# One load queue with a fixed order for two SwiGLU output stages, block sums loaded in the gate stage, four subtractions on GpSimd

## The chip, the cores and the metric

The kernel runs on one core of a Trainium2 chip. Five engines of the core work side by side, each with its own list of instructions: TensorE (PE in the profile, with PEld for its weight loads), VectorE (DVE), ScalarE (ACT), GpSimd (POOL) and SyncE (SP), which here only issues transfers. An instruction waits until the semaphores that it names are reached, and what stands behind it on the same engine waits with it. DMA transfers can be issued by SyncE and by ScalarE too; on either, an issue is a row of that engine's list, and the profile calls the two lists SPq and ACTq. The metric is the device time of one execution in microseconds (us).

## The reference, cut to what matters

The program is one decoder block on 1040 tokens (16 learned ones ahead of 1024) of width 1024, all in float32: a half-step SwiGLU, a mixer of two branches, a second half-step SwiGLU, and a final norm.

```python
def _swiglu(x, w_gu, w_down):              # w_gu (1024, 5632), w_down (2816, 1024)
    gate, up = jnp.split(x @ w_gu, 2, axis=-1)
    return (jax.nn.silu(gate) * up) @ w_down

h = h + 0.5 * _swiglu(_rmsnorm(h, ffn1_norm), ffn1_w_gu, ffn1_w_down)
u = _rmsnorm(h, mix_norm)                  # the mixer's input
...                                        # the mixer: h = h + merged @ w_out
h = h + 0.5 * _swiglu(_rmsnorm(h, ffn2_norm), ffn2_w_gu, ffn2_w_down)
return _rmsnorm(h, final_norm)[:, N_META:]
```

The change touches the last product of each SwiGLU, `(silu(gate) * up) @ w_down`, and the step from the first of them to the norm `u` of the mixer.

## The kernel before, in words

The kernel keeps activations transposed: a tile has 128 channels on its partitions and tokens along the row. The residual stream h is 8 such tiles, called h0 to h7 (hh0 to hh7 in the second SwiGLU).

**Precision.** A float32 product is made from three reduced ones. `split` (L162 to L164) writes a high part of a tile on ScalarE (L163) and the rest, source minus high part, on VectorE (L164, a subtraction with two inputs in the core's memory). Three matmuls, high by high, high by low and low by high, are summed in PSUM. Weights and activations are both split, so each weight tile costs ScalarE and VectorE one instruction each, and so does each activation tile.

**Stages.** The first SwiGLU has a gate stage (about 20 to 474 us of the span) and an output stage (474.6 to 717.5 us); then follows the mixer, called `middle`, whose first matmul starts at 721.9 us. The second SwiGLU has its gate stage up to 2781.8 us and its output stage from there to 3013 us; the final norm ends at 3028.2 us.

**The output stage.** `down` multiplies with a scheme that needs 7 products of half-size matrices where 8 are usual. A round r (0 to 6) is one of the 7. Its activation factor is one of the 7 forms in `FORMS` (t4, t1, t2, b22, b11, t3, b21), made of 11 tiles; its weight factor is a block of w_down or a sum of blocks, 4 row blocks m of 11 tiles of 128x128 each, in two chunks of 6 and 5 tiles (768 and 640 columns). So a round is 4 products, and a product has 66 matmuls in the first SwiGLU (two column halves of 256 and 264 tokens) or 33 in the second (512 tokens). At the end of a product VectorE adds the result to one or more h tiles (L707, "h add" below).

**Block sums.** The buffer `wsum` holds one round's weight factor for all four m. Rounds 0 and 4 load a block of w_down straight into it. Rounds 1, 2, 3 and 5 load another block into one of two buffers `wraw`, and GpSimd adds or subtracts it into `wsum` (L241). Round 6 needs a plain block and uses `wraw` alone; so does row block 0 of round 0. `loadw` then splits the chunk into a tile `w` for TensorE, and `fetchw` starts a load some chunks ahead of its use. A program written out once (`weight_order`) fixes the order of the chunks.

**Forms.** The gate stage makes the 7 forms of each of 11 tile columns k and stores them in device memory (`frm`, L523). The output stage brings them back, into slots that earlier rounds have used: `Hidden.load` issues the loads (L674, on ScalarE's list), `Hidden.split` splits them (L163 and L164 again), and `Hidden.step` says before each product how far both may go. A slot is free once the last product of the round that read it has used it. The very last form of the gate stage is split straight from the tile that holds it (`direct`), without a trip through memory.

**Residual.** `residuals` loads the h tiles, 260 KB halves, ahead of products of round 0 and, for four of them, of round 3 (L815 in the first SwiGLU, L925 in the second), on SyncE, as are the weights.

**What sets the order.** Each engine's list is fixed when the program is built. The order in which the Python code issues instructions is one input; a scheduler then places each instruction, and `issue_after` pins one instruction behind another. Before, the weight loads are chained to each other so, and the residual and `wsum` loads are pinned behind a weight load, while the form loads stand where the scheduler puts them on ScalarE's list, between the splits. Transfers of SyncE and ScalarE share eight completion semaphores in turn, so that each transfer's issue also waits for the one eight before it, from whichever list that came.

**The switch.** Behind the last round of the first SwiGLU, `hooks.after` squares h for the norm's sum (ACT L319, added up by GpSimd into `nsq`, L326), makes the normed tiles `nt` (DVE L866, two buffers) and splits each into `uk`, the mixer's input (`u_tile`). The mixer's first projection then reads `uk` (tile `pp`, L306), and a column sum over `nsq` on TensorE (`nps`, L337) belongs to the norm of the second half of the tokens.

Of the kernel before, what the change touches and what calls it, by code (L numbers as in the profile page):

```python
# [13 lines left out]
P = 128  # L14
# [202 lines left out]

def down_weights(g, name, raw, r, m, k0, kk):

    blk = lambda i, j: g.a[name][m + HK * i][:, HF * j + k0 : HF * j + k0 + kk]  # L220

    def dma(t, i, j):
        with ExitStack() as behind:
            if g.wdma and t is not raw:
                behind.enter_context(g.tc.issue_after(g.wdma.ins))
            ins = g.nc.sync.dma_start(t, blk(i, j))
        if t is raw:
            g.wdma = ins

    if r == LAST or (r == 0 and m == 0):  # L230
        dma(raw, *((0, 1) if r else (1, 1)))
        return raw
    s = g.wsum[:, m, k0 : k0 + kk]
    if r in (0, 4):
        dma(s, r == 0, r == 0)
        return s
    if r == 1 and m == 0:
        dma(s, 1, 1)
    dma(raw, *((1, 0), (0, 0), (0, 1), None, (1, 0))[r - 1])
    x, y = (raw, s) if r == 3 else (s, raw)  # L240
    g.nc.gpsimd.tensor_tensor(s, x, y, op=ALU.add if r == 1 else ALU.subtract)  # L241
    return s


def fetchw(g):
# [6 lines left out]
    if not down or idx[0] not in (0, 4) or idx[:2] == (0, 0):  # L252
        raw = g.wp.tile([P, KD, P], F32, name="wraw", tag="wraw", bufs=2)[:, :kk]
# [367 lines left out]
class Hidden:  # L621


    def __init__(self, g, n, pools):
        self.g, self.n, self.pools, self.loads, self.at = g, n, pools, [], {}
        self.order = [(r, p) for r in range(len(FORMS)) for p in range(HF)]
# [9 lines left out]
    def ahead(self):  # L636
        g = self.g
        g.wcount, g.wdma, g.held, g.direct = 0, None, [], self.direct
# [5 lines left out]
        fetchw(self.g)  # L644
# [6 lines left out]
        yield  # L651
        self.split(8)
        yield
        fetchw(self.g)
        self.split(HF - 1)
        yield
# [10 lines left out]
    def load(self, upto, done):  # L667
        while len(self.loads) < min(upto, len(self.slots)):
# [4 lines left out]
            if i != HF - 1:  # L673
                self.g.nc.scalar.dma_start(t[:, 1, :].bitcast(F32), self.g.frm[rp][:, : self.n])  # L674
# [13 lines left out]
def down(g, hs, which, n, hidden, hooks):  # L688
# [20 lines left out]
    for r in range(len(FORMS)):  # L709
        cols = halves(n)  # L710
        kept = {}
        for m in range(HK):
            hidden.step(r, m)
            hooks.before(r, m)

            def w(k0):
                kept[m, k0] = loadw(g, f"wdn{which}", r, m, k0)
                return kept[m, k0]
# [42 lines left out]
def ffn1(g):  # L761
    tc, nc = g.tc, g.nc
    n = T // 2
    with ExitStack() as ctx:
# [31 lines left out]
        hidden = Hidden(g, n, pools)  # L796
        g.wthird = ctx.enter_context(tc.tile_pool(name="wd", bufs=1, reuse_waits="tile"))
# [5 lines left out]
        hs = {k: sp.tile([P, T], F32, name=f"h{k}") for k in (3, 7, 2)}  # L803
        sum_tile = lambda shape, dtype: sp.tile(shape, dtype, name="wsum", tag="wsum", bufs=1)
        g.wsum = sum_tile([P, HK, HF, P], F32)
        hs.update({k: sp.tile([P, T], F32, name=f"h{k}") for k in (6, 5, 1, 0, 4)})
        spare = sp.tile([P, 2, ROW(n)], F32R, name="form")[:, :, :n]
        hidden.odd = hidden.places("t3", "22", "t4", "t1")
        hidden.arrange(spare, [])
        hooks = K()  # L810

        def residual(k, half):
            sl = slice(half * n, half * n + n)
            with tc.issue_after(g.wdma.ins):
                nc.sync.dma_start(hs[k][:, sl], g.a["hT"][k][:, sl])  # L815
# [3 lines left out]
        def before_last():  # L819
            early.close()  # L820
            t = sum_tile([P, 5, 2, ROW(n)], F32R)
# [8 lines left out]
            with tc.issue_after(g.wdma.ins):  # L830
                nc.sync.dma_start(g.ck, g.a["ck"][:, P:NSB])
# [18 lines left out]
        def after(r, m, s):  # L850
# [13 lines left out]
            for k, rs in hooks.todo[: 2 * s]:  # L864
                t = g.un.tile([P, 528], F32, name="nt", tag="nt", bufs=2)
                nc.vector.scalar_tensor_tensor(t, hs[k][:, SEGS[0][0] :], g.V("gm", k), rs, op0=ALU.mult, op1=ALU.mult)  # L866
                g.u.append(u_tile(g, t))
# [7 lines left out]
def ffn2(g):  # L875
# [3 lines left out]
    with ExitStack() as ctx:  # L879
# [28 lines left out]
        hidden = Hidden(g, n, pools)  # L908
        g.wthird = ctx.enter_context(tc.tile_pool(name="wd", bufs=1, reuse_waits="tile"))
# [4 lines left out]
        hs = {k: sp.tile([P, SEQ], F32, name=f"hh{k}") for k in (3, 7, 2)}  # L914
        g.wsum = sp.tile([P, HK, HF, P], F32, name="wsum", tag="wsum", bufs=1)
        hs.update({k: sp.tile([P, SEQ], F32, name=f"hh{k}") for k in (6, 5, 1, 0, 4)})
# [996 lines left out]
```

## Time and profile before

| | us |
|---|---|
| median of 3 runs | 3026.28 (3025.98 to 3031.26) |
| the profiled execution | 3030.14 |
| its span, first to last instruction | 3028.2 |
| PE busy in it | 2895.7 (96%) |
| DVE, ACT, POOL busy | 2165.3, 1438.0, 480.2 |
| first output stage, to the mixer's first matmul | 474.6 to 721.9 |
| second output stage | 2781.8 to 3013 |

The profiled execution is 3.9 us over the median, so differences are formed against its own time and then set off from the median. Instruction times count from the start of the span. Two columns of the stretch table matter most: how long PE was busy in a stretch, and PEclk, the mean clock that was granted to it (1.00 is full). "Idle before" in the timeline is the time for which an engine stood ahead of that instruction, with the instruction or transfer that ended it. A row of SPq or ACTq is a transfer's issue with the time for which it held its list; what it waits for holds up everything behind it there.

### The profile page before, as it was taken

The numbers are of one execution on the slowest core, as the hardware profiler recorded it, in microseconds if no ns is written. First come the engines' busy times: TensorE is split into PE (matmuls) and PEld (weight loads), VectorE is DVE, ScalarE is ACT, GpSimd is POOL, SyncE is SP. The second block draws the span as 40 slices with busy tenths as digits, with TensorE's granted clock in tenths as the row PEclk, the third lists the DMA queues.
The fourth block names the chain that finished last, engine by engine and source line by source line (L and its number), as shares of the span: only waits on it lengthen the run. The fifth ranks groups of instructions, "written<-read, shape, count | busy, mean of one in ns | idle before, by whom it ended". The sixth has DMA issues, their size and how long they took to land.

```text
span 3028.2 us, 62795 instructions
## 1 busy us (share of the span) xinstructions
PE 2895.7 (96%) x25630; PEld 2505.8 (83%) x25630; DVE 2165.3 (72%) x4083; ACT 1438.0 (47%) x2546; POOL 480.2 (16%) x550
## 2 busy tenths in 40 slices
PE   8999998999989999999998999999999999999998
PEld 8999998999877888888776777777777788887786
DVE  6566665866677877778868888777866766667675
ACT  5322223436655656556565655665644432224334
POOL 0332331412000000000000110000000033331520
PEclk9999999999999999999999999999999999999999
DMA  3333247644232322333332333233354233336662
GB/s 119 98 106 106 93 136 240 209 135 128 74 74 66 85 70 69 74 81 98 81 93 66 85 87 76 76 75 86 106 153 161 79 104 105 105 104 212 226 186 91
DMA packets 289727, 334.57 MB, mean 110 GB/s; under 512 B 172752, under 2 KB 178896, under 8 KB 289440
## 3 DMA queue, kind: packets, MB, share of 16 engines
q1 hardware_dynamic: 265744, 287.05, 31.8%
q10 hardware_dynamic: 23616, 43.33, 4.4%
q8 instruction: 201, 3.29, 0.5%
q14 instruction: 86, 0.70, 0.1%
q0 software_dynamic: 80, 0.19, 0.0%
HBM read 263.11 MB, written 67.38 MB: 109 GB/s over the span
## 4 chain that ended last, share of the span: by engine, by line
PE 46%; DVE 12%; ACT 5%; DMA 3%; issue 2%; POOL 1%; SPq 1%; DVEq 0%; ACTq 0%; POOLq 0%
PE pp L306 14%; PE pg L493 12%; PE pd L700 4%; PE pwo L306 3%; DVE w L164 2%; DVE tb L1575 1%; PE pg L517 1%; DVE Xb L1577 1%; ACT w L163 1%; DMA wraw<-in_wdn 1%; PE cs L1207 1%; PE vp L1260 1%; PE mp L1260 1%; DVE mt L1683 1%; PE np L1260 1%
## 5 line engine op out<-in xcount | busy, mean ns | idle before, releaser
L306 PE MATMUL pp<-uk,w 128*128 128x512 f32 (+2 forms) x4824 | 968.2, 346 | 13.8 <-DVE w L164 5.7
L306 PEld LDWEIGHTS pp<-uk,w 128*128 128x128 f32 x4824 | 742.5, 190 | 110.8 <-DVE w L164 13.0
L700 PE MATMUL pd<-form,w 128*128 128x256 f32 (+2 forms) x2652 | 432.0, 325 | 26.6 <-ACT w L163 14.7
L700 PEld LDWEIGHTS pd<-form,w 128*128 128x128 f32 x2652 | 388.3, 192 | 69.0 <-ACT w L163 15.5
L164 DVE TENSOR_TENSOR w<-wraw,w 128x1024 fp32r<-128x1024 f32 (+2 forms) x270 | 352.9, 1307 | 83.5 <-ACT w L163 79.9
L493 PE MATMUL pg<-bt,w 128*128 128x256 f32 (+2 forms) x2520 | 400.8, 317 | 0.2 <-DVE w L164 0.2
L493 PEld LDWEIGHTS pg<-bt,w 128*128 128x128 f32 x2520 | 360.2, 188 | 33.3 <-DVE w L164 0.6
L163 ACT ACTIVATE w<-wraw 128x1024 fp32r<-128x1024 f32 (+2 forms) x270 | 279.8, 1036 | 208.0 <-PE pg L493 127.7
L499 DVE TENSOR_TENSOR c<-c,pg 128x520 f32<-128x520 f32 (+1 forms) x280 | 189.4, 688 | 237.1 <-PE pg L493 213.0
L493 PE MATMUL pg<-b,w 128*128 128x256 f32 (+2 forms) x2160 | 347.8, 317 | 0.0
L493 PEld LDWEIGHTS pg<-b,w 128*128 128x128 f32 x2160 | 309.7, 188 | 28.1
L163 ACT ACTIVATE w<-wrx 128x1024 fp32r<-128x1024 f32 (+1 forms) x64 | 58.4, 912 | 281.5 <-PE pg L493 239.3
L163 ACT ACTIVATE w<-wsum 128x768 fp32r<-128x768 f32 x92 | 72.7, 791 | 228.1 <-PE pd L700 145.7
L463 POOL TENSOR_TENSOR wrx<-wrx 128x512 f32<-128x512 f32 x38 | 52.5, 1382 | 726.8 <-DVE w22b L164 548.9
L164 DVE TENSOR_TENSOR w<-wsum,w 128x768 fp32r<-128x768 f32 x92 | 95.9, 1048 | 85.7 <-ACT w L163 85.7
L1577 DVE TENSOR_TENSOR Xb<-Xb,tb 115x126 f32<-115x126 f32 (+22 forms) x496 | 125.2, 252 | 9.1 <-DVE tb L1575 0.4
L1575 DVE TENSOR_TENSOR tb<-Ub,Xb 115x126 f32<-115x126 f32 (+22 forms) x496 | 123.9, 250 | 9.3 <-DMA Ub<-scr 2.2
L1384 DVE SCALAR_TENSOR_TENSOR acc<-xr,pk,acc 128x528 f32<-128x528 f32 (+1 forms) x144 | 108.9, 757 | 29.3 <-ACT acc L1380 28.7
L241 POOL TENSOR_TENSOR wsum<-wsum,wraw 128x768 f32<-128x768 f32 (+1 forms) x48 | 93.2, 1955 | 229.1 <-DMA wsum<-in_wdn 106.6
L164 DVE TENSOR_TENSOR form<-form 128x512 fp32r<-128x512 f32 (+1 forms) x147 | 125.6, 900 | 2.0 <-ACT form L163 2.0
L306 PE MATMUL pwo<-uk,w 128*128 128x512 f32 x384 | 99.6, 412 | 4.1 <-DVE w L164 1.9
L163 ACT ACTIVATE form<-form 128x512 fp32r<-128x512 f32 (+1 forms) x147 | 83.0, 622 | 27.6 <-DMA form<-frm 11.6
(427 smaller groups left out, 4416.7 us busy)
## 6 DMA issues: line engine op xcount, KB each, us to landing
wraw<-in_win SPq DMA_DIRECT2D x150, 512.0 KB
wraw<-in_wgu SPq DMA_DIRECT2D x44, 512.0 KB
wrx<-in_wgu SPq DMA_DIRECT2D x44, 512.0 KB
frm<-c SPq DMA_DIRECT2D x76, 260.0 KB
frm<-c SPq DMA_DIRECT2D x76, 256.0 KB
form<-frm ACTq DMA_DIRECT2D x76, 256.0 KB
form<-frm ACTq DMA_DIRECT2D x71, 260.0 KB
wraw<-in_wdn SPq DMA_DIRECT2D x42, 384.0 KB
```

Source lines behind the costliest of these rows:

```text
L163: g.nc.scalar.activation(hi, src, AF.Copy)
L164: (eng or g.nc.vector).tensor_tensor(lo, src, hi.bitcast(F32), op=ALU.subtract)
L241: g.nc.gpsimd.tensor_tensor(s, x, y, op=ALU.add if r == 1 else ALU.subtract)
L306: g.nc.tensor.matmul(ps, lhsT=l, rhs=r, start=i == 0, stop=i == n - 1)
L463: sums.tensor_tensor(a22, a21, a22, op=ALU.add)
L493: nc.tensor.matmul(ps[:, c0 : c0 + cn], lhsT=l[:, x, k, :], rhs=r[:, k, y, c0 : c0 + cn], start=i == 0, stop=i == 3 * HK - 1)
L499: nc.vector.tensor_tensor(o, x, y, op=ALU.add)
L700: nc.tensor.matmul(pd[:, c0 : c0 + cn], lhsT=wd[:, u, k - k0, :], rhs=x[:, v, c0 : c0 + cn], start=k + i == 0, stop=k == HF - 1 and i == 2)
L1260: g.nc.tensor.matmul(ps[e][HS[dst], c0 : c0 + CB], lhsT=l, rhs=r, start=True, stop=True)
L1384: nc.vector.scalar_tensor_tensor(acc[:, :n], xr[:, tap : tap + n], V("convw", ct * 4 + tap), acc[:, :n], op0=ALU.mult, op1=ALU.add)
L1575: nc.vector.tensor_tensor(tv, U[:, i, i + 1 :].unsqueeze(2).to_broadcast([npt, nt, ncc]), X[:, i, 0:ncc].unsqueeze(1).to_broadcast([npt, n ...
L1577: nc.vector.tensor_tensor(X[:, i + 1 :, 0:ncc], X[:, i + 1 :, 0:ncc], tv, op=ALU.add)
```

## The change

1. A new helper `in_turn` issues a transfer from SyncE and pins it behind the one that it issued before. Within the output stages all loads go through it: the weights, the residual tiles, and the forms, which leave ScalarE's list. With this, 152 load rows leave ScalarE; SyncE's list is 1305 instead of 1173 rows. The order in which the code asks for the loads is now their order on the chip; the residual loads of a product come behind both weight chunks that are fetched in it.
2. `wsum` gets a pool of its own ("ws"), opened before the gate stage's inner part and no longer in the output stage's pool. `ahead`, which runs inside the gate stage, loads the four row blocks of round 0 into it, each as one transfer of 128x1408 (704 KB) instead of two. Row block 0 of round 0 is read from `wsum` too. Round 4 loads whole row blocks as well.
3. The pool of the third split weight tile ("wd") opens after the output stage's pool; the extra forms of the first SwiGLU's last round and the final norm's tiles take their room from the new pools.
4. At the switch the low parts of `uk` for odd k (4 of 8) are subtracted on GpSimd instead of VectorE.

The matmuls and their number stay as they were.

How this moves rows is seen at three places. The first is SyncE's list at the start of the first output stage, from the last store of a form on (`h_5068` and the like are h tiles; one load brings half of its tokens). Before:

```order
L523 DMA frm<-c_4920 128x520
L815 DMA h_5068<-in_hT 128x520
L815 DMA h_5065<-in_hT 128x520
L815 DMA h_5067<-in_hT 128x520
L815 DMA h_5068<-in_hT 128x520
L226 DMA wsum<-in_wdn 128x768
L226 DMA wsum<-in_wdn 128x640
L815 DMA h_5064<-in_hT 128x520
L815 DMA h_5066<-in_hT 128x520
L815 DMA h_5065<-in_hT 128x520
L226 DMA wsum<-in_wdn 128x768
L226 DMA wsum<-in_wdn 128x640
```

With the change, from the third row behind the last store on:

```order
L223 DMA h_5068<-in_hT 128x520
L223 DMA form<-frm 128x520 x3
L223 DMA h_5064<-in_hT 128x520
L223 DMA h_5066<-in_hT 128x520
L223 DMA h_5065<-in_hT 128x520
L223 DMA form<-frm 128x520 x3
L223 DMA h_5062<-in_hT 128x520
L223 DMA h_5063<-in_hT 128x520
L223 DMA h_5064<-in_hT 128x520
L223 DMA form<-frm 128x520 x2
L223 DMA wraw<-in_wdn 128x768
L223 DMA wraw<-in_wdn 128x640
```

The `wsum` loads are gone from here (they stand in the gate stage), form loads stand in their place, and the first `wraw` load of round 1 comes behind 18 residual and form loads.

The second place is ScalarE's list in rounds 0 and 1 of the same stage. Before:

```order
L163 ACTIVATE w<-wsum 128x640
L674 DMA form<-frm 128x520 x4
L163 ACTIVATE w<-wsum 128x768
L674 DMA form<-frm 128x520
L163 ACTIVATE form<-form 128x520 x4
L674 DMA form<-frm 128x520
```

With the change:

```order
L163 ACTIVATE w<-wsum 128x640
L163 ACTIVATE form<-form 128x520 x4
L163 ACTIVATE w<-wsum 128x768
L163 ACTIVATE form<-form 128x520 x2
L163 ACTIVATE w_5470<-wsum 128x640
L163 ACTIVATE form<-form 128x520 x2
```

The loads are gone from between the splits; the splits of four forms now stand ahead of the next chunk's split of weights.

The third place is VectorE's list at the switch, from the second normed tile on (`w<-wraw` is a weight of the mixer). Before:

```order
L866 SCALAR_TENSOR_TENSOR nt<-h_5066,pk,nrs 128x528
L164 TENSOR_TENSOR w<-wraw,w 128x1024
L164 TENSOR_TENSOR uk<-nt,uk 128x528 x2
L707 SCALAR_TENSOR_TENSOR h_5066<-pd,h_5066 128x256
L866 SCALAR_TENSOR_TENSOR nt<-h_5062,pk,nrs 128x528
L866 SCALAR_TENSOR_TENSOR nt<-h_5060,pk,nrs 128x528
L164 TENSOR_TENSOR uk<-nt,uk 128x528 x2
L866 SCALAR_TENSOR_TENSOR nt<-h_5068,pk,nrs 128x528
L707 SCALAR_TENSOR_TENSOR h_5062<-pd,h_5062 128x256
```

With the change, VectorE:

```order
L871 SCALAR_TENSOR_TENSOR nt<-h_5066,pk,nrs 128x528
L164 TENSOR_TENSOR w<-wraw,w 128x1024
L164 TENSOR_TENSOR uk<-nt,uk 128x528
L714 SCALAR_TENSOR_TENSOR h_5066<-pd,h_5066 128x256
L871 SCALAR_TENSOR_TENSOR nt<-h_5063,pk,nrs 128x528
L871 SCALAR_TENSOR_TENSOR nt<-h_5061,pk,nrs 128x528
L164 TENSOR_TENSOR uk<-nt,uk 128x528
L871 SCALAR_TENSOR_TENSOR nt<-h_5068,pk,nrs 128x528
L871 SCALAR_TENSOR_TENSOR nt<-h_5065,pk,nrs 128x528
L714 SCALAR_TENSOR_TENSOR h_5063<-pd,h_5063 128x256
```

and GpSimd, where the subtractions have gone between the sums of squares:

```order
L327 TENSOR_TENSOR nsq<-nsq 128x512 x4
L164 TENSOR_TENSOR uk<-nt,uk 128x528
L327 TENSOR_TENSOR nsq<-nsq 128x512
L164 TENSOR_TENSOR uk<-nt,uk 128x528 x2
L327 TENSOR_TENSOR nsq<-nsq 128x512
L164 TENSOR_TENSOR uk<-nt,uk 128x528
```

VectorE keeps every second low part; a normed tile `nt` that takes the buffer of an odd one now waits for GpSimd.

The diff, cut to what these points speak of:

```diff
+def in_turn(g, out, src):
+
+    with ExitStack() as behind:
+        if g.turn:
+            behind.enter_context(g.tc.issue_after(g.turn.ins))
+        g.turn = g.nc.sync.dma_start(out, src)
+
+
+def block(g, name, m, i, j, k0=0, kk=HF):
+    return g.a[name][m + HK * i][:, HF * j + k0 : HF * j + k0 + kk]
+
+
 def down_weights(g, name, raw, r, m, k0, kk):
 
-    ...
-    if r == LAST or (r == 0 and m == 0):
-        dma(raw, *((0, 1) if r else (1, 1)))
+    s = g.wsum[:, m, k0 : k0 + kk]
+    if r == 4 and k0 == 0:
+        in_turn(g, g.wsum[:, m], block(g, name, m, 0, 0))
+    if raw is None:
+        return s
+    i, j = ((1, 0), (0, 0), (0, 1), None, (1, 0), (0, 1))[r - 1]
+    in_turn(g, raw, block(g, name, m, i, j, k0, kk))
+    if r == LAST:
         return raw
-    s = g.wsum[:, m, k0 : k0 + kk]
-    if r in (0, 4):
-        dma(s, r == 0, r == 0)
-        return s
-    if r == 1 and m == 0:
-        dma(s, 1, 1)
-    dma(raw, *((1, 0), (0, 0), (0, 1), None, (1, 0))[r - 1])
     x, y = (raw, s) if r == 3 else (s, raw)
     g.nc.gpsimd.tensor_tensor(s, x, y, op=ALU.add if r == 1 else ALU.subtract)
     return s
...
     def ahead(self):
         g = self.g
-        g.wcount, g.wdma, g.held, g.direct = 0, None, [], self.direct
+        g.wcount, g.turn, g.held, g.direct = 0, None, [], self.direct
+        sums = lambda m: g.nc.sync.dma_start(g.wsum[:, m], block(g, self.name, m, 1, 1))
...
+        sums(0)
+        fetchw(g)
         self.split(3)
...
+        sums(1)
         self.split(8)
         yield
-        fetchw(self.g)
+        fetchw(g)
         self.split(HF - 1)
+        for m in (2, 3):
+            sums(m)
         yield
...
             if i != HF - 1:
-                self.g.nc.scalar.dma_start(t[:, 1, :].bitcast(F32), self.g.frm[rp][:, : self.n])
+                in_turn(self.g, t[:, 1, :].bitcast(F32), self.g.frm[rp][:, : self.n])
...
             hidden.step(r, m)
-            hooks.before(r, m)
 
             def w(k0):
                 kept[m, k0] = loadw(g, f"wdn{which}", r, m, k0)
+                if k0:
+                    hooks.before(r, m)
                 return kept[m, k0]
...
-        g.wthird = ctx.enter_context(tc.tile_pool(name="wd", bufs=1, reuse_waits="tile"))
+        wp = ctx.enter_context(tc.tile_pool(name="ws", bufs=1, reuse_waits="tile"))
+        g.wsum = wp.tile([P, HK, HF, P], F32, name="wsum", tag="wsum", bufs=1)
         with tc.tile_pool(name="gs", bufs=1, reuse_waits="tile") as sp:
             gu.send((hidden.ahead(), sp))
...
         hidden.arrange(spare, [])
+        g.wthird = ctx.enter_context(tc.tile_pool(name="wd", bufs=1, reuse_waits="tile"))
...
-                g.u.append(u_tile(g, t))
+                g.u.append(u_tile(g, t, nc.gpsimd if k % 2 else None))
...
-def u_tile(g, src):
+def u_tile(g, src, eng=None):
...
-    split(g, src, uk[:, 0, :], uk[:, 1, :])
+    split(g, src, uk[:, 0, :], uk[:, 1, :], eng)
     return uk
```

49 lines of the change are left out of this document (18 added, 31 removed).

## The prediction

> **What bounds the kernel now.** I read three views in turn: busy time by stretch (where does TensorE stop being busy?), its waits in those stretches (what ended them?), and the timeline at each (what was late, and for whom?). First the stretches of the two output stages; columns: length, PE busy with matmuls, PEld, DVE, ACT, POOL, granted clock, DMA share, GB/s.
>
> ```profile
> 474.50:520.00 45.50, 37.76 (x295) 36.85 (x294) 25.12 (x34) 14.68 (x23) 9.30 (x6) 0.92 0.82 290
> 520.00:560.00 40.00, 34.54 (x258) 33.80 (x257) 27.87 (x27) 12.03 (x19) 24.96 (x13) 0.91 0.65 201
> 560.00:600.00 40.00, 40.00 (x336) 40.00 (x336) 33.17 (x41) 19.27 (x32) 12.43 (x7) 1.00 0.71 237
> ...
> 2780.00:2820.00 40.00, 32.99 (x133) 26.30 (x132) 24.14 (x36) 15.48 (x24) 8.05 (x4) 0.87 0.88 305
> 2820.00:2860.00 40.00, 35.60 (x148) 28.30 (x147) 26.21 (x26) 11.11 (x18) 23.66 (x13) 0.96 0.65 208
> 2860.00:2900.00 40.00, 38.00 (x166) 30.65 (x165) 34.08 (x39) 16.84 (x28) 15.34 (x8) 1.00 0.73 231
> 2900.00:3013.00 113.00, 113.00 (x496) 92.71 (x495) 77.99 (x102) 48.25 (x73) 18.70 (x10) 1.00 0.38 120
> ```
>
> TensorE is the bound wherever it is full, and nothing here shortens a full stretch. Only the first 85 us of the first stage and the first 120 us of the second have idle time and a low clock. Full stretches also give the pace: 40.00/336 x 66 matmuls = 7.9 us per product of the first stage, 113.00/496 x 33 = 7.5 us in the second; a round of four is 31.5 and 30 us. TensorE's waits, 474 to 740 us, then 2780 to 3028 us:
>
> ```profile
> PE pd L700 <- ACT w L163: 7.6, 2, 6.3
> PE pd L700 <- DVE w L164: 4.5, 4, 2.5
> PE pp L306 <- DVE h L707: 4.4, 1, 4.4
> PE pd L700 <- ACT form L163: 0.8, 1, 0.8
> PE pd L700 <- DVE form L164: 0.4, 1, 0.4
> ```
>
> ```profile
> PE pd L700 <- ACT w L163: 7.0, 1, 7.0
> PE pd L700 <- DVE w L164: 6.4, 5, 3.1
> ```
>
> So 13.3 us of idle time in the first stage, 4.4 at the switch and 13.4 in the second. The timeline names what each stands for:
>
> ```profile
> 489.84 0.84 ACT L163 ACTIVATE w<-wsum 128x768 fp32r<-128x768 f32 x1 [5.50 <-DMA wsum<-in_wdn]
> 490.72 0.96 DVE L164 TENSOR_TENSOR w<-wsum,w 128x768 fp32r<-128x768 f32 x1 [4.96 <-ACT w L163]
> 490.74 0.80 PE L700 MATMUL pd<-form,w 128*128 128x256 f32 x2 [6.27 <-ACT w L163]
> ...
> 513.47 11.69 ACTq L674 DMA_DIRECT2D form<-frm  x4
> 525.28 0.84 ACT L163 ACTIVATE w<-wsum 128x768 fp32r<-128x768 f32 x1 [11.13 <-PE pd L700]
> 526.18 0.51 PE L700 MATMUL pd<-form,w 128*128 128x256 f32 x2 [1.38 <-ACT w L163]
> 528.29 3.11 PE L700 MATMUL pd<-form,w 128*128 128x256 f32 x16 [1.61 <-DVE w L164]
> 548.52 3.78 PE L700 MATMUL pd<-form,w 128*128 128x256 f32 x20 [2.47 <-DVE w L164]
> ...
> 2796.52 1.78 PE L700 MATMUL pd<-form,w 128*128 128x512 f32 x3 [7.01 <-ACT w L163]
> 2839.01 6.83 DVE L164 TENSOR_TENSOR form<-form 128x512 fp32r<-128x512 f32 x4
> 2846.63 8.68 PE L700 MATMUL pd<-form,w 128*128 128x512 f32 x30 [3.08 <-DVE w L164]
> ```
>
> The second product of round 0 waits in both stages for a block's transfer, 6.27 and 7.01 us. The stalls at 526 and 528 us come from ScalarE: four form loads held its list from 513.47 for 11.69 us, so the next weight split ran at 525.28. (The view puts that wait down to TensorE; 525.16 is where the fourth load was issued.) Those at 548 and 2846 us have another look: VectorE is late, and four form splits there took 6.83 us. Each stall is also paid in clock:
>
> ```profile
> 490.70:495.10 4.40, 4.17 (x18) 3.87 (x19) 2.70 (x4) 2.51 (x5) 0.00 (x0) 0.51 1.03 381
> 526.00:533.00 7.00, 5.21 (x28) 5.00 (x29) 6.24 (x7) 3.64 (x8) 4.25 (x3) 0.76 0.77 225
> 548.00:553.10 5.10, 4.58 (x25) 4.58 (x26) 3.72 (x5) 0.00 (x0) 4.56 (x2) 0.67 0.25 70
> 2796.50:2802.40 5.90, 5.88 (x14) 4.33 (x15) 4.97 (x7) 4.33 (x7) 0.00 (x0) 0.50 0.92 317
> 2834.00:2851.00 17.00, 12.60 (x46) 9.50 (x46) 17.00 (x16) 5.62 (x10) 12.07 (x7) 0.90 0.52 157
> ```
>
> Length times (1 - clock) is what the low clock cost: 2.2, 1.7, 1.7, 2.95 and 1.7 us. The Trainium skill (TensorE: Matmul & The Clock Gate, "What's actually happening") puts the half clock after about one idle window of some 3.4 us. The trace is stricter, since 2.47 us of idle at 548 us sufficed; by the page the sum below would lack the clock terms of the shorter stalls, about 3.4 us, and I go by the rows.
>
> **The change part by part.** *Block sums in the gate stage.* Round 0 no longer waits for its weights: 6.3 + 0.2 us in the first stage (the 0.2 is the next weight chunk's wait on VectorE) and 7.0 in the second, with 2.2 and 2.95 of clock. What it adds is four transfers of 704 KB early in the gate stage, 2.8 MB, some 10 us at the 290 GB/s above. That is hidden by slack there:
>
> ```profile
> DMA  3333247644232322333332333233354233336662
> L493 PE MATMUL pg<-bt,w 128*128 128x256 f32 (+2 forms) x2520 | 400.8, 317 | 0.2 <-DVE w L164 0.2
> ```
>
> The DMA engines are three tenths busy in the first slices (75.7 us each), and TensorE lost 0.2 us over 2520 matmuls of gate products. Without that cover a gate weight would come up to 10 us late, once per stage; below nothing is impossible, as the stage has no wait to win. I take 0.
>
> *The direct form.* The 0.8 + 0.4 us at the first stage's start come from ScalarE being busy with loads and form splits there. Its list is shorter now, but the form is still made last: between 0 and -1.2, I take -0.4.
>
> *Form loads off ScalarE.* The 1.4 + 1.6 us at 526 and 528 go, with 1.7 of clock, if the loads on SyncE don't hold what is needed sooner. At the stage's start SyncE issues 18 residual and form loads (each 128x520 floats; 4.8 MB together) ahead of round 1's first block: 16 us at 290 GB/s, from some 4 us into the stage on, so the block lands near 496, is added by 499 and split by 501; round 1 begins at 474.6 + 31.5 = 506. Slack 5 us, in the second stage some 4. Later, four form loads for round r+1 stand ahead of the weights and wait for the first tiles of round r's last product; the split of the weights for r+1's second product stands behind the splits of these forms on ScalarE. From the first freed slot to that product is 15.8 us (two products; 15 in the second stage). Needed: 2.9 us until four of eleven tiles are read, 2.5 for loads, 4 x 0.62 for ScalarE's splits, one VectorE split, then 0.84 + 0.96 for the weights, together some 10.4. Slack about 5 us again.
>
> *Who shares with whom.* VectorE and GpSimd hinder each other, and rounds 1, 2, 3 and 5 use both:
>
> ```profile
> 2841.48 1.87 POOL L241 TENSOR_TENSOR wsum<-wsum,wraw 128x768 f32<-128x768 f32 x1 [0.98 <-DMA wraw<-in_wdn]
> 2788.63 3.09 DVE L164 TENSOR_TENSOR form<-form 128x512 fp32r<-128x512 f32 x5
> ```
>
> A form split is 0.62 us alone and 1.71 us (6.83/4) beside GpSimd's sums. If they exclude each other, a round holds 4 x (1.87 + 1.56) on GpSimd (640 columns by five sixths), 4 x (0.96 + 0.80) of weight splits and 11 x 0.62 of forms: 13.7 + 7.0 + 6.8 = 27.5 us of 31.5 or 30. That fits, but tightly, and a late start isn't caught up. The stretch 560 to 600 us, with 33.17 of VectorE and TensorE full, says that it can go well; 2860 to 2900 us, with 34.08 and 2 us lost, that it need not. So of the stalls of this kind, 2.5 us at 548 and 6.4 in the second stage, I take half: 1.2 and 3.2, and half of their clock, 0.85 each. Bounds: none and all.
>
> *Four low parts to GpSimd.* At the switch TensorE waits for VectorE:
>
> ```profile
> 717.62 0.69 DVE L164 TENSOR_TENSOR uk<-nt,uk 128x528 fp32r<-128x528 f32 x1
> 718.01 1.44 POOL L326 TENSOR_TENSOR nsq<-nsq 128x512 f32<-128x512 f32 x1 [3.20 <-issue]
> 718.35 1.68 DVE L866 SCALAR_TENSOR_TENSOR nt<-h,pk,nrs 128x528 f32<-128x528 f32 x1
> 720.68 0.77 DVE L866 SCALAR_TENSOR_TENSOR nt<-h,pk,nrs 128x528 f32<-128x528 f32 x1
> 721.37 0.42 DVE L707 SCALAR_TENSOR_TENSOR h<-pd,h 128x256 f32<-128x256 f32 x1
> 721.93 4.19 PE L306 MATMUL pp<-uk,w 128*128 128x272 f32 x17 [4.43 <-DVE h L707]
> ```
>
> A normed tile takes 0.77 us alone and 1.68 beside GpSimd's addition, which takes 1.44. So a low part on GpSimd, 1.4 us by that row, shuts VectorE out, where it took 0.69 there: 4 x 0.7 = +2.8 if all is in series, less what the h adds (0.42, one input in PSUM) overlap. If they ran side by side, 4 x 0.69 = 2.8 would be won. The normed tiles, with two buffers, also wait for GpSimd now. The 0.91 us by which nt was longer decides for the first: +2.2. The Trainium skill says so too (SBUF — State Buffer, "SBUF: two separate sides": the pair of ports is an exclusive lock for a whole instruction); by it alone the term is the +2.8. The wait of 4.4 grows to some 6.6; late behind it is the mixer's first projection, which TensorE has nothing else to put before.
>
> *The sum.* First stage 6.5 + 0.4 + 3.0 + 1.2 + 2.2 + 1.7 + 0.85 = 15.9; second 7.0 + 3.2 + 2.95 + 0.85 = 14.0; switch -2.2. Together 27.7 us less: 3030.14 - 27.7 = 3002.4 for an execution like the profiled one, which is 3.9 us over the median of the runs: 2998.5.
>
> **The rivals.** *Rounds 1 and 2 keep their stalls*, since VectorE and GpSimd exclude each other and the form splits come no earlier. For it: 6.83 us for four splits. Against it: 560 to 600 us. Then only 6.5 + 2.2 + 7.0 + 2.95 - 2.8 = 15.9 are won: 3010. *Everything comes back*: all stalls and clock of both stages (18.8 and 18.1), the switch 2 us better, because GpSimd's work falls into VectorE's pauses: 39 less, 2987. Against it stands the nt row. *SyncE becomes the bound, and the kernel slower*: the four form loads wait for round r's last product, everything behind them with them, and the 5 us of slack are used up at each of five later rounds of both stages, for instance as VectorE's splits grow to 1.71 us and GpSimd's sums queue behind late blocks. A stall of 4 us with 1.7 of clock, ten times, is 57 against some 26 won: 3057. It decides above about 2.6 us a round; the slack worked out above speaks against it. *The sums come early but the gate stage pays*, with 5 us and clock in each: 3012; the 0.2 us row and the idle DMA engines speak against it. *The early sums don't land in time* because the buffer's room is freed late: round 0 waits as before and the rest gains 12 less 2: 3016.
>
> **How the numbers follow.** Forecast 0.52, stalls kept 0.17, all back 0.13, SyncE bound and slower 0.08, gate stage pays 0.06, sums late 0.04. The time is that of the first, 2998.5. The main case's own bounds are 2987 to 3010; with some microseconds of spread between runs and the middle rivals I go from 2985 to 3014. 0.2% is 6 us, about what a measurement tells from no change. Faster by more: all but the slower case and a part of the two middle ones, 0.87. Within 6 us: 0.05. Slower: 0.08.
>
> **What would show it.** Right: `w` splits of round 0 with no wait on a `wsum` transfer, TensorE full from 480 to 506 us, the ACTq rows of `form<-frm` gone and the stall at 526 us with them, clock 1.00 through 520 to 560 us, `uk<-nt` on POOL at about 1.4 us each, `pp` about 2 us later behind the last product. Wrong: waits for `wraw` or `form` on SPq's transfers in rounds 1 to 5, a gate stage that ends later than 474.6, or a switch that is shorter than 4.4 us.

## The result and the profile after

The changed kernel takes 3008.05 us (median of 5 runs, 3005.43 to 3014.11) where the kernel before took 3026.28: a ratio of 0.9939, 95% interval 0.9923 to 0.9955, so 18 us less with an interval of some 14 to 23. The forecast was 2998.5; the time lies in its range and the gain is two thirds of the one forecast. The profiled execution took 3009.62 us, its span is 3007.6 (before: 3028.2).

Where the 20.6 us between the two spans come from, by the first and last matmuls of the tiles pg, pd, pp and pwo (the mixer's last product) in both timelines (us); the second gate stage counts from the last pwo matmul, the mixer from the first of pp:

| stretch | before | after | difference | forecast |
|---|---|---|---|---|
| start and first gate stage | 474.6 | 473.9 | -0.7 | 0 |
| first output stage | 242.9 | 234.4 | -8.5 | -15.9 |
| switch, to the first pp matmul | 4.4 | 6.0 | +1.5 | +2.2 |
| mixer | 1630.9 | 1632.3 | +1.4 | 0 |
| second gate stage | 429.0 | 431.3 | +2.3 | 0 |
| second output stage | 231.2 | 214.7 | -16.5 | -14.0 |

The mixer is all but the same program in all kernels here, and in the fourteen profiles it took between 1628.8 and 1635.2 us (by the granted clock, 16 to 25 us of that were lost to half clock, more in one execution than in another); so a total that differs by 3 to 5 us says little, and most verdicts below go by the stretch that an edit touches.

TensorE's waits in the changed kernel, 474 to 740 us and then 2760 to 3010 us:

```profile
PE pd L707 <- DVE w L164: 7.2, 6, 2.3
PE pp L307 <- DVE h L714: 6.0, 1, 6.0
PE nps L338 <- POOL nsq L327: 0.8, 1, 0.8
PE pd L707 <- ACT w L163: 0.7, 2, 0.4
```

```profile
PE pd L707 <- DVE w L164: 2.0, 4, 0.7
PE pg L494 <- DVE w L164: 0.7, 1, 0.7
PE nps L338 <- ACT fin L320: 0.6, 1, 0.6
```

The long waits on ScalarE (7.6 and 7.0 us before) are gone in both stages. What is left of pd's waits is nearly all VectorE: 6.4 fell to 2.0 in the second stage, but 4.5 rose to 7.2 in the first. The stretches of the first stage (same columns as before):

```profile
474.50:520.00 45.50, 45.50 (x380) 45.30 (x379) 36.53 (x40) 20.01 (x31) 15.23 (x9) 1.00 0.85 285
520.00:560.00 40.00, 37.37 (x297) 36.96 (x296) 33.97 (x31) 13.75 (x20) 20.16 (x10) 0.96 0.49 156
560.00:600.00 40.00, 37.88 (x317) 37.67 (x316) 31.13 (x36) 13.79 (x21) 12.08 (x6) 1.00 0.51 182
600.00:640.00 40.00, 39.58 (x331) 39.38 (x330) 34.19 (x40) 18.40 (x28) 16.25 (x8) 1.00 0.68 227
640.00:680.00 40.00, 39.35 (x328) 39.31 (x328) 22.94 (x33) 14.88 (x23) 1.52 (x2) 1.00 0.48 159
```

The first 45.5 us are full at clock 1.00, as the forecast said. But 520 to 560 us still has a hole, and 560 to 680 us, which was full before, now has some too. The largest one, in the timeline of TensorE, VectorE and GpSimd around it:

```profile
519.77 2.43 DVE L164 TENSOR_TENSOR w<-wsum,w 128x768 fp32r<-128x768 f32 x1
522.12 4.93 DVE L164 TENSOR_TENSOR form<-form 128x520 fp32r<-128x520 f32 x3
526.97 2.15 DVE L164 TENSOR_TENSOR w<-wsum,w 128x640 fp32r<-128x640 f32 x1
...
519.54 4.08 POOL L242 TENSOR_TENSOR wsum<-wsum,wraw 128x768 f32<-128x768 f32 x2 [2.07 <-DMA wraw<-in_wdn]
524.56 1.93 POOL L242 TENSOR_TENSOR wsum<-wsum,wraw 128x768 f32<-128x768 f32 x1 [0.94 <-DMA wraw<-in_wdn]
526.78 1.66 POOL L242 TENSOR_TENSOR wsum<-wsum,wraw 128x640 f32<-128x640 f32 x1 [0.29 <-DMA wraw<-in_wdn]
...
518.32 0.72 ACT L163 ACTIVATE w<-wsum 128x640 fp32r<-128x640 f32 x1
...
529.18 1.06 PE L707 MATMUL pd<-form,w 128*128 128x256 f32 x5 [2.35 <-DVE w L164]
```

ScalarE is on time here: it began the high part of the 640-column chunk at 518.32, 8.65 us before VectorE began the low part. VectorE is behind: its weight splits take 2.43 and 2.15 us, and three form splits 4.93, each time beside a sum of GpSimd.

### The profile page after: what moved, and what is told of

The parts are those of the page before. It is cut to its first block, busy times and chain, and to the rows that moved or that the text cites. A ratio compares the mean times of both kernels' runs of the same rounds, so it can differ in the third digit from the quotient of the medians.

```text
span 3007.6 us, 62829 instructions
## 1 busy us (share of the span) xinstructions
PE 2890.0 (96%) x25630; PEld 2501.7 (83%) x25630; DVE 2194.8 (73%) x4079; ACT 1445.0 (48%) x2546; POOL 491.2 (16%) x554
## 4 chain that ended last, share of the span: by engine, by line
PE 50%; DVE 12%; ACT 5%; issue 2%; DMA 1%; SPq 0%; POOL 0%; DVEq 0%; ACTq 0%
PE pp L307 16%; PE pg L494 11%; PE pd L707 6%; PE pwo L307 3%; DVE w L164 2%; DVE tb L1581 1%; PE pg L518 1%; DVE Xb L1583 1%; ACT w L163 1%; PE cs L1213 1%; PE vp L1266 1%; PE mp L1266 1%; DVE mt L1689 1%; PE gra L1467 1%; PE np L1266 1%
## 5 line engine op out<-in xcount | busy, mean ns | idle before, releaser
L707 PEld LDWEIGHTS pd<-form,w 128*128 128x128 f32 x2772 | 396.7, 190 | 49.9 <-DVE w L164 12.3
L164 DVE TENSOR_TENSOR form<-form 128x520 fp32r<-128x520 f32 (+1 forms) x152 | 145.1, 991 | 13.0 <-ACT form L163 12.7
L164 DVE TENSOR_TENSOR w<-wsum,w 128x768 fp32r<-128x768 f32 x96 | 116.0, 1214 | 36.8 <-ACT w L163 36.8
L163 ACT ACTIVATE form<-form 128x520 fp32r<-128x520 f32 (+1 forms) x152 | 94.2, 632 | 77.1 <-DMA form<-frm 67.7
```

What stands on the lines that cost most here:

```text
L163: g.nc.scalar.activation(hi, src, AF.Copy)
L164: (eng or g.nc.vector).tensor_tensor(lo, src, hi.bitcast(F32), op=ALU.subtract)
L707: nc.tensor.matmul(pd[:, c0 : c0 + cn], lhsT=wd[:, u, k - k0, :], rhs=x[:, v, c0 : c0 + cn], start=k + i == 0, stop=k == HF - 1 and i == 2)
```

## The experiments

The theory at this point: VectorE and GpSimd exclude each other whenever both read their inputs from the core's memory; the first stage's remaining stalls, the longer switch, and a part of the old stalls that the forecast had put down to the form loads on ScalarE are all this one thing. The single rows of VectorE speak for it already: of 63 form splits of the first stage up to 680 us, 47 took 0.68 to 0.70 us and 16 took 1.91 to 2.35, with none between. So a split ran at its own pace there or was held up by most of a sum. The rivals: transfers that are late on SyncE's one list; the order of splits on VectorE; too few weight tiles.

**The same kernel once more**

> The changed kernel itself, as the base for the other three on this chip and to see how much its stretches differ between two executions. If the stalls of rounds 1 to 5 depend on how GpSimd's sums and VectorE's splits happen to meet, the first output stage differs by some microseconds from the 234.4 us of its first profile, with the stalls at other places; if they are set by the order of the loads alone, it repeats within 1 us. The time should be within 0.3% of 3008.

3013.2 us (3008.81 to 3015.08), ratio 0.9957 (0.9944 to 0.9970). The first output stage took 234.2 us, as before, but the stalls lay elsewhere: 2.03 us at 558, 1.00 at 634, 2.64 at 638 and only 0.31 at 526. The second took 212.2 (214.7). So the stage's length repeated, against what the theory expected of it, while the places moved, as it expected. That the length came out the same is chance: two kernels below whose rounds 1 to 5 are the same (low parts back on VectorE; early loads spread) took 237.8 and 240.4 us for the stage, with stalls of the same kind near 526 to 530, 562 to 565 and 634 to 645 us. The order of the loads, the same in all of them, doesn't set the stage's length by itself.

**GpSimd writes, but reads nothing**

```diff
-    g.nc.gpsimd.tensor_tensor(s, x, y, op=ALU.add if r == 1 else ALU.subtract)
+    for t in (raw, s, raw):
+        g.nc.gpsimd.memset(t, 0.0)
```

> The changed kernel with GpSimd's block sums replaced by three writes of zeros to the same tiles (about as long, but nothing is read, so the sums are left out). If the stalls left in the first output stage (2.35 us at 526.8, 2.12 at 562.6, 1.06 at 639.6) and the 2.0 us in the second come from VectorE and GpSimd excluding each other when both read, VectorE's splits are all 0.62 to 0.96 us, these stalls fall to under 1 us in all, and the time falls by 6 to 10 us. If they come from forms or blocks that land late on the one list of loads, or from too few weight tiles, they stay above 4 us.

This kernel leaves the sums out, so what it computes is of no use; its one execution took 3000.19 us. The first output stage falls from 234.4 to 227.5 us, the second from 214.7 to 211.4, and TensorE has no wait at all in rounds 1 to 5 of either; what stays, 2.7 us, is in the last round. The groups of the first stage, changed kernel and then this one (busy us, mean ns of one, idle before):

```profile
L164 DVE TENSOR_TENSOR form<-form 128x520 fp32r<-128x520 f32 x64 | 65.5, 1058 | 4.5 <-ACT form L163 4.4
L164 DVE TENSOR_TENSOR w<-wsum,w 128x768 fp32r<-128x768 f32 x23 | 29.6, 1288 | 0.8 <-ACT w L163 0.8
L242 POOL TENSOR_TENSOR wsum<-wsum,wraw 128x768 f32<-128x768 f32 x12 | 24.8, 2064 | 106.5 <-DMA wraw<-in_wdn 71.4 <-DVE h L714 31.5 <-DVE form L164 3.6
```

```profile
L164 DVE TENSOR_TENSOR form<-form 128x520 fp32r<-128x520 f32 x63 | 41.9, 696 | 7.5 <-ACT form L163 7.1
L164 DVE TENSOR_TENSOR w<-wsum,w 128x768 fp32r<-128x768 f32 x23 | 21.9, 952 | 1.7 <-ACT w L163 1.7
L243 POOL MEMSET wraw<- 128x768 f32 x32 | 23.7, 741 | 31.1 <-DMA wraw<-in_wdn 30.2
```

A form split takes 696 ns on average where it took 1058, a weight split 952 instead of 1288, although GpSimd is as busy as before (three writes of 741 ns for a sum of 2064). All 63 form splits up to 680 us now take 0.69 or 0.70 us; the group of 1.91 to 2.35 is gone. So neither GpSimd's time nor the loads are the cause, but what it reads. This is what the Trainium skill says (SBUF — State Buffer, "SBUF: two separate sides"): an instruction of VectorE with two inputs in that memory is locked out only by a GpSimd instruction that reads there.

**The sums on VectorE**

```diff
-    g.nc.gpsimd.tensor_tensor(s, x, y, op=ALU.add if r == 1 else ALU.subtract)
+    g.nc.vector.tensor_tensor(s, x, y, op=ALU.add if r == 1 else ALU.subtract)
```

> The changed kernel with all block sums on VectorE instead of GpSimd. If exclusion is what costs the stalls of rounds 1 to 5, a sum holds the shared inputs for 0.80 or 0.96 us instead of 1.57 or 1.87, VectorE and GpSimd need 20.8 instead of 27.5 us of a round in turn, and the idle time of both output stages falls from 8 and 0.2 to 2 us to about 3 (the last round's) and under 1; the first stage falls to some 229 us. If VectorE was the bound by its own work, with GpSimd beside it for free, its list grows by 7 us a round and the stalls grow to 10 us or more in each stage.

3001.36 us, ratio 0.9918 (0.9905 to 0.9931). The output stages take 227.1 and 211.4 us, no wait of TensorE is left in rounds 1 to 5, and 2.1 us in the last round; these are all the waits of pd, in the first stage (the second has none):

```profile
PE pd L707 <- ACT w L163: 1.7, 1, 1.7
PE pd L707 <- DVE w L164: 0.5, 1, 0.5
```

VectorE got 16 sums of 768 columns and 16 of 640 more to do, and still came to wait for others:

```profile
L164 DVE TENSOR_TENSOR form<-form 128x520 fp32r<-128x520 f32 x64 | 42.8, 694 | 5.0 <-ACT form L163 4.6
L164 DVE TENSOR_TENSOR w<-wsum,w 128x768 fp32r<-128x768 f32 x23 | 21.8, 950 | 1.1 <-ACT w L163 1.1
L242 DVE TENSOR_TENSOR wsum<-wsum,wraw 128x768 f32<-128x768 f32 x12 | 11.4, 952 | 2.6 <-DMA wraw<-in_wdn 2.5
```

A sum takes 952 ns there against 2064 on GpSimd. The engine that was said to be late gets more work and is on time: that settles exclusion as the cause, and with it that the loads of SyncE's list are not late in these rounds, since they stayed as they were.

**Form loads back on ScalarE**

```diff
-                in_turn(self.g, t[:, 1, :].bitcast(F32), self.g.frm[rp][:, : self.n])
+                self.g.nc.scalar.dma_start(t[:, 1, :].bitcast(F32), self.g.frm[rp][:, : self.n])
```

> The changed kernel with the form loads back on ScalarE's list; block sums stay early and all other loads stay in SyncE's fixed order. If holding ScalarE was what cost 3.0 us of idle time and 1.7 of clock at 526 us, these come back, the second output stage gets its 1.3 to 3 us back too, and the time rises by 5 to 9 us over the changed kernel. If the exclusion of VectorE and GpSimd sets those stalls whichever list the loads are on, both output stages stay within 2 us of the changed kernel's.

3016.97 us, ratio 0.9968 (0.9958 to 0.9977). Both theories are half right. The first output stage takes 233.6 us, not a microsecond more than with the loads on SyncE; ScalarE's stall comes back (1.64 us at 480, 2.56 at 516), but VectorE's go down by as much. The second takes 222.8 us, 8 to 11 more than in the two profiles of the changed kernel, with these waits (2775 to 2995 us):

```profile
PE pd L707 <- DVE w L164: 6.7, 6, 3.1
PE pd L707 <- ACT w L163: 0.7, 1, 0.7
```

Three stalls of TensorE there, 0.59, 3.08 and 1.53 us, are those of the kernel before to the hundredth, ahead of the same matmuls of the stage (the 201st, 219th and 366th); in the changed kernel none of the three is there. So in that stage VectorE was late because of the list that the form loads stood on. In microseconds the list's worth is less sure. With the loads on SyncE and the sums on GpSimd the second stage took 212.2 to 220.0 us in eight profiles, which makes it 3 to 11 us there; in the medians on the same chip it is 3.8 us (3013.2 to 3016.97), and the intervals of the two ratios overlap. In the first stage it is worth nothing, as long as GpSimd makes the sums. Why that stage gives it all back was not separated further, and form loads on ScalarE with the sums on VectorE were not run.

**Form splits behind the weights**

```diff
-            split(self.g, t[:, 1, :].bitcast(F32), t[:, 0, :], t[:, 1, :])
+            split(self.g, t[:, 1, :].bitcast(F32), t[:, 0, :], t[:, 1, :], after=self.g.wlow)
```

> The changed kernel with VectorE's part of each form split pinned behind the weight split that was used last, so that form splits no longer stand ahead of weights that are needed sooner. If the stalls of the first output stage come from that order under exclusion, 526.8 and 562.6 us fall to under 0.5 us each and the time falls by 3 to 6 us. If VectorE and GpSimd together are simply full in rounds 1 to 3, the stalls move to the forms and the time stays within 1.5 us.

3006.34 us, ratio 0.9951 (0.9933 to 0.9969). The stalls at 526 and 562 us became 1.50 and 1.62 us, a new one of 2.43 came in the second stage; the stages take 232.5 and 215.0 us. Against the changed kernel (0.9939 and 0.9957) this is no difference: splitting the forms behind the weights doesn't remove the stalls, they move.

**Low parts back on VectorE**

```diff
-                g.u.append(u_tile(g, t, nc.gpsimd if k % 2 else None))
+                g.u.append(u_tile(g, t))
```

> The changed kernel with the four low parts of the normed tiles back on VectorE. If the pair GpSimd and VectorE lengthens the switch, TensorE's wait ahead of the mixer's first matmul falls from 5.96 to about 4.4 us, the 0.76 us ahead of nps go, and the time falls by 2 to 3 us. If the longer switch comes from the new order of loads and stores instead, the wait stays near 6 us and the time within 1 us.

3003.5 us, ratio 0.9939 (0.9923 to 0.9956). The ratio is the changed kernel's own, so the total doesn't show the 2 to 3 us that were expected: in the profile the first output stage came out 3.4 us longer (237.8), in rounds that the edit doesn't touch. The switch itself does: it takes 4.1 instead of 6.0 us and the wait of nps is gone, 2.7 us together. In the changed kernel two normed tiles near the end of the switch took 3.40 us beside GpSimd's low part and sum; with the low parts on VectorE, two tiles at the same place took 1.68 and 0.77, the first of them still beside a sum:

```profile
709.50 1.35 POOL L164 TENSOR_TENSOR uk<-nt,uk 128x528 fp32r<-128x528 f32 x1 [2.00 <-ACT uk L163]
709.73 3.40 DVE L871 SCALAR_TENSOR_TENSOR nt<-h,pk,nrs 128x528 f32<-128x528 f32 x2
710.81 1.76 POOL L327 TENSOR_TENSOR nsq<-nsq 128x512 f32<-128x512 f32 x1
...
714.23 2.15 PE L307 MATMUL pp<-uk,w 128*128 128x272 f32 x8 [5.96 <-DVE h L714]
```

```profile
711.63 1.45 POOL L327 TENSOR_TENSOR nsq<-nsq 128x512 f32<-128x512 f32 x1 [3.20 <-issue]
711.96 1.68 DVE L871 SCALAR_TENSOR_TENSOR nt<-h,pk,nrs 128x528 f32<-128x528 f32 x1
...
714.30 0.77 DVE L871 SCALAR_TENSOR_TENSOR nt<-h,pk,nrs 128x528 f32<-128x528 f32 x1
...
715.54 4.19 PE L307 MATMUL pp<-uk,w 128*128 128x272 f32 x17 [4.05 <-DVE h L714]
```

**Early block loads spread over the gate stage**

```diff
-        sums = lambda m: g.nc.sync.dma_start(g.wsum[:, m], block(g, self.name, m, 1, 1))
+        def sums(m):
+            with g.tc.issue_after(g.gateloads[int(self.name[-1]), 4 + m, 0].ins):
+                g.nc.sync.dma_start(g.wsum[:, m], block(g, self.name, m, 1, 1))
```

> The changed kernel with the four early block loads of a stage pinned one each behind the weight loads of four later gate units. If the second gate stage's new stalls (0.47 and 0.72 us at 2408) come from two block loads that share the DMA engines with a gate weight, they go, the gate stage is 1 to 2 us shorter, and the first gate stage stays as it is. If they come from the buffers' new place, they stay.

What they are to move shows in the changed kernel's second gate stage:

```profile
2400.95 0.33 SPq L454 DMA_DIRECT2D wraw<-in_wgu  x1
2401.34 0.90 SPq L641 DMA_DIRECT2D wsum<-in_wdn  x2
...
2406.40 1.06 ACT L163 ACTIVATE w<-wraw 128x1024 fp32r<-128x1024 f32 x1 [3.22 <-DMA wraw<-in_wgu]
...
2408.46 0.73 PE L494 MATMUL pg<-bt,w 128*128 128x512 f32 x2 [0.47 <-ACT w L163]
...
2409.91 1.43 PE L494 MATMUL pg<-bt,w 128*128 128x512 f32 x5 [0.72 <-DVE w L164]
```

The same step in the kernel before:

```profile
2407.25 0.33 SPq L453 DMA_DIRECT2D wraw<-in_wgu  x1
...
2410.83 1.06 ACT L163 ACTIVATE w<-wraw 128x1024 fp32r<-128x1024 f32 x1 [1.35 <-DMA wraw<-in_wgu]
```

The gate weight, issued at 2400.95, could be split only at 2406.40, 5.45 us later, with two blocks of 704 KB on the DMA engines beside it; before, it took 3.58 us. With the loads spread, both waits are gone, one of 0.74 us stays (it is in the changed kernel too, at 2764, when forms are split), and the stage takes 430.0 instead of 431.3 us. Over all profiles the gain is smaller: 429.8 to 430.1 us in the five runs with this edit, 430.4 to 431.3 in the eight without it. The total, 3010.31 us with a ratio of 0.9952 (0.9935 to 0.9970), doesn't show it: in the profiled execution, the slowest of ten, the first gate stage came out 1.7 us longer (in the later runs with this edit it is as in the changed kernel) and the output stages 6.0 and 5.3 us, with the same lists there, through stalls of the kind above.

**The last round**

> The changed kernel with the squares of h4 to h7 for the mixer's norm made one pair per product of the last round instead of all eight ahead of it. If the four stalls at 680 to 687 us (2.1 us together) come from the last round's weight splits standing behind squares that wait for GpSimd, they fall to under 0.5 us; if the weights land late there, they stay at about 2 us. The switch may grow by some tenths, since the sums end later.

```diff
-            for s in range(2):
-                for k in range(HK, KD):
-                    squares(s, k)
...
             squares(s, m)
+            if not s:
+                squares(0, m + HK)
+                squares(1, m + HK)
```

The four stalls went, but nps then waited 3.61 us, because the first half's sum ended later: 3013.24 us in one run, nothing won. All four edits together, with this one:

> The changed kernel with four edits together: low parts of the normed tiles on VectorE, early block loads spread over the gate stage, form splits pinned behind used weights, squares spread over the last round. By the terms that the runs showed so far: switch 2.6 us less, second gate stage 1.3 less, last round 2 less with its clock, rounds 1 to 3 some 1 to 2 less, together 6 to 8 us under the changed kernel. If the stalls only move between VectorE and GpSimd, it is within 3 us of the kernel with the low parts on VectorE alone (3003.5).

3009.28 us, ratio 0.9939 (0.9926 to 0.9953): the switch took 2.9 us, but nps waited 3.96, and rounds 1 to 3 kept 2.9 us of stalls. The expected 6 to 8 us were missed. A third form moved only the squares that GpSimd sums:

```diff
-            for s in range(2):
-                for k in range(HK, KD):
-                    squares(s, k)
+            for k in range(HK, KD):
+                squares(0, k)
...
             squares(s, m)
+            if not s:
+                squares(1, m + HK)
```

> The changed kernel with three edits: low parts of the normed tiles on VectorE, early block loads spread over the gate stage, and only those squares of h4 to h7 that GpSimd sums spread over the last round. The stalls at 680 to 687 us fall to under 0.7 us with no stall at nps, the switch is 4 us, the second gate stage 1.3 us shorter: together 5 to 6 us under the changed kernel. If the last round's stalls were not GpSimd's squares, only 3 to 4 us.

3008.47 us, ratio 0.9942 (0.9928 to 0.9956). The last round kept 2.2 us of stalls (1.37 and 0.82): a weight split took 1.40 us beside a GpSimd sum of 1.28 there. The expected 5 to 6 us under the changed kernel were missed too: the ratio is the changed kernel's (0.9939) within 0.0003. Moving GpSimd's sums about within the round doesn't help. All runs with GpSimd's sums on it and the form loads on SyncE, from 3003.5 to 3013.2 us, lie within 10 us of each other, and the mixer alone spreads by 6.

**What the cause allows: nothing on GpSimd that reads**

> The three edits of the run before and the block sums on VectorE. If exclusion holds, some 10 us under the changed kernel; if VectorE is full with the sums, slower than the run with three edits by 5 us or more.

The edits are those of the run with three and the sums on VectorE, as shown above. 2994.15 us, ratio 0.9894 (0.9880 to 0.9908).

```diff
-            hooks.rms = [Rms(..., add_on=nc.gpsimd if s else None) ...]
+            hooks.rms = [Rms(..., add_on=None) ...]
```

> The four edits of the run before and the mixer's norm sums on VectorE too, so that GpSimd reads nothing in the first output stage. If exclusion is what lengthens VectorE's splits in the last round (1.40 us for a weight split beside GpSimd's sum), its stalls fall from 2.3 to about 1 us and the time by 1 to 2 us. If the last round waits for the squares on ScalarE's list instead, the stalls stay near 2 us and the time is the same within its interval.

2990.16 us, ratio 0.9877 (0.9860 to 0.9893): 36 us under the kernel before, twice the gain of the change. The output stages take 226.6 and 211.4 us. The last round's stalls fell from 2.3 to 1.5 us, and, not expected, the switch from 4.0 to 1.1 us. In the run with four edits, near the switch, a pair of low parts took 2.31 us (696.71) and a pair of normed tiles 2.44 (701.87), each beside a sum of GpSimd; here such pairs take 1.32 and 1.44, and VectorE makes its own sums in between:

```profile
699.24 1.32 DVE L164 TENSOR_TENSOR uk<-nt,uk 128x528 fp32r<-128x528 f32 x2
...
700.48 0.76 DVE L876 SCALAR_TENSOR_TENSOR nt<-h,pk,nrs 128x528 f32<-128x528 f32 x1
...
701.49 0.76 DVE L876 SCALAR_TENSOR_TENSOR nt<-h,pk,nrs 128x528 f32<-128x528 f32 x1
701.72 2.22 PE L307 MATMUL pp<-uk,w 128*128 128x272 f32 x16 [1.14 <-DVE h L718]
```

## Why the prediction was right, and where its terms were not

The direction, the range and most mechanisms held. That the two output stages together came within 5 us of the forecast is in part luck: the first gave 7.4 us less than its sum and the second 2.5 us more, and not for the reasons booked. Term by term:

- **Block sums in the gate stage**: right. No split of round 0 waits for a block; the 6.5 and 7.0 us are gone with their clock, and 474.5 to 520 us is full. Its cover was priced at 0 from the DMA engines' mean share and the 0.2 us of lost time. That held in the first gate stage and failed in the second, which took 2.3 us longer: about 1 us where a gate weight had no slack beside two block loads, and 0.74 at 2764, where a form split stands ahead of a weight's split. Spreading the loads gave back 0.3 to 1.5 us. A mean share says nothing of two transfers that meet.
- **The direct form**: its 1.2 us went altogether; 0.4 was forecast.
- **Form loads off ScalarE**: SyncE's order had slack, as was worked out, since with the sums on VectorE and the same list of loads TensorE waits for nothing in rounds 1 to 5. It was less than the 5 us given: the 2.5 us for four form loads has no row beside it, and in the changed kernel 4.2 to 4.4 us passed from their first issue to their first split (500.47 to 504.65, 505.88 to 510.18, 512.03 to 516.42). But its term in the first stage (3.0 us and 1.7 of clock) was booked in full, and this step failed. The rows were read rightly as ScalarE being held for 11.69 us; what would be late next, VectorE, was counted only under the next term. Idle time in rounds 1 to 5 was 5.5 us before and 5.8 after; only clock was won there, and the sign of being right that named clock 1.00 from 520 to 560 us did not come (0.96). In the second stage the sum had no term for these loads at all. It put the stalls there down to VectorE and GpSimd, and the run with the loads back on ScalarE brings the same stalls back: they needed the loads on ScalarE too.
- **Who shares with whom**: the 27.5 us of exclusive work per round of 31.5 was the right sum, and "half" the wrong choice for the first stage, where none came back and the last round added 2.1 us; in the second, 4.4 of 6.4 us came back instead of half, because the form loads had left ScalarE. The 1.71 us "beside GpSimd's sums" was a mean of unlike rows: the four splits took 2.04, 0.68, 2.33 and 2.02 us. The rival in which rounds 1 and 2 keep their stalls (3010) describes the first stage. Its time is nearer to the measured one than the forecast's, but by chance: it left the second stage's stalls in place too, and had nothing for the gate stage.
- **Low parts to GpSimd**: +2.2 forecast, +1.5 at the switch and 0.8 at nps measured; the run with them on VectorE gives back 2.7. The nt row was the right one to go by.
- **The slower case**, SyncE as the bound, showed nowhere.

Together: the output stages gave 25.0 us where 29.9 were forecast, and the second gate stage took 2.3 that weren't in the sum; the rest is the switch with nps, the mixer's spread and the start.

## What to carry to other kernels

When a stall is put down to one engine, work out what the next engine in the chain could do if the first were on time, before the whole stall is booked as a gain. Where VectorE makes two-input operations all the time, an addition on GpSimd is not free: in its shortest rows, where it hadn't to wait for VectorE itself, it took 1.84 us (2.06 on average), of which VectorE could use next to none for such work, against 0.95 on VectorE, so the sum of both engines' times, not the larger of them, is what has to fit in a round. Price a load that is moved under cover at the tightest moment of the cover, not by its mean.

## What the runs showed that was not expected

GpSimd instructions that only write did not slow VectorE's two-input operations (952 and 696 ns, as in the run with no sums on GpSimd: 950 and 694), while those that read did. Casts of 128x128 are another matter: in the changed kernel, beside GpSimd's low part and then its zero writes, one took 2.31 and one 1.46 us; with GpSimd idle at that point, in the last run, 0.23 and 0.22. In the run with four edits the second one took 4.37 us (706.33), beside a sum and then a row of zero writes that followed each other without a pause. No run changed these writes alone.

```profile
714.28 2.31 DVE L1022 CAST onesr<-ones 128x128 fp32r<-128x128 f32 x1
715.14 1.37 POOL L1006 MEMSET Y<- 128x1536 f32 x1
715.20 1.46 DVE L1022 CAST bdr<-ck 128x128 fp32r<-128x128 f32 x1
```

```profile
704.28 0.23 DVE L1027 CAST onesr<-ones 128x128 fp32r<-128x128 f32 x1
...
704.42 0.22 DVE L1027 CAST bdr<-ck 128x128 fp32r<-128x128 f32 x1
```

And the clock: a stall of 2.35 us at 526.8 was followed by a stretch at clock 0.73, one of 2.12 us at 562.6 by none (changed kernel, same columns as above). Between stalls of this size the price in clock can't be told from their length alone. What decides shows in the times at which the granted clock changes: in each of the fourteen profiles they lie, within 0.04 us, on a grid of 3.41 us (each profile has a grid of its own). The stall of 2.35 us fell inside one such stretch; that of 2.12 us fell on two, 1.21 us in one and 0.91 in the next. The second profile of the changed kernel has the pair within one execution: 2.03 us at 558, inside one stretch, cost half clock for the next one, while 2.64 us at 638, cut into 1.81 and 0.83, cost none. In all fourteen profiles, between 25 and 2980 us of the span, every stretch at full clock in which TensorE was idle for 2.0 us or more was followed by half clock; with less idle time some were and most were not. So a stall that the forecast priced with 1.7 us of clock may cost that or nothing, by where it falls on the grid, and that differs from one execution to the next.

```profile
526.80:533.10 6.30, 3.96 (x21) 3.93 (x21) 5.14 (x6) 0.62 (x1) 1.64 (x1) 0.73 0.00 0
562.00:567.00 5.00, 2.88 (x24) 2.67 (x23) 5.00 (x6) 0.74 (x1) 1.67 (x1) 1.00 0.04 13
```
